# The first layer's gates by expert: built by token through DRAM before the stream, instead of by chunks between its tiles

## The chip, the core and the metric

The kernel runs on one core of a Trainium2 chip. The metric is the device time of one execution in microseconds (us), here the median of three runs. The core's engines work side by side, each through a fixed order of its own instructions: TensorE (PE; its loads of weights are PEld), VectorE (DVE), ScalarE (ACT), GpSimd (POOL) and SyncE (SP), which only starts transfers. An instruction starts when the one before it on its engine is done and when the semaphores that it waits for are set.

## The reference, cut to what matters

Two layers are computed on 256 latent tokens (LAT) and 256 context tokens (CTX) of width 1024. A layer is a mixer (a projection, a gated delta rule as a scan, pooling and Fourier groups) and then a retrieval of experts, to which the change belongs:

```python
def _peer(h, w_query, sub_keys, expert_u, expert_v):
    q = (h @ w_query).reshape(t, 8, 2, 128)
    scores = einsum('thpc,hpnc->thpn', q, sub_keys)
    s_top, i_top = top_k(scores, 16)
    cand = s_top[:, :, 0, :, None] + s_top[:, :, 1, None, :]
    cand_idx = i_top[:, :, 0, :, None] * 128 + i_top[:, :, 1, None, :]
    best, pos = top_k(cand.reshape(t, 8, 256), 16)
    idx = take_along_axis(cand_idx.reshape(t, 8, 256), pos)
    gate = softmax(best)
    act = gelu(einsum('td,thkd->thk', h, expert_u[idx]))
    return einsum('thk,thkd->td', gate * act, expert_v[idx])
```

So each token has 8 x 16 = 128 chosen experts out of 128 x 128. An expert's number is a pair of keys, the first and the second, 128 of each. In the first layer both kinds of tokens retrieve; the last layer gives only the latents.

## The kernel before

The two kinds of tokens retrieve in different ways.

**Context, by gathers.** `gather_rows` fetches, for each of the 128 choices and each block of 128 tokens, the rows of u and v of each token's expert (256 gathers of 1 MB). POOL starts an indirect DMA into a buffer `uv` (L966); VectorE multiplies the u half by h and sums it to `dots` (L975); ScalarE applies gelu and the gate; VectorE adds the v half times `dots` to `acc` (L986). Of the products with h, 19 are done by POOL instead and summed by ScalarE (`PST`, `PMOD`, L971). The buffers are UVA = 3, and UVB = 1 more for the first UVN = 100 gathers.

**Latents, densely.** `stream` goes over all 128 x 128 experts in 128 tiles, one for each first key. For each it loads the tile's u and v from DRAM (0.5 MB each, SP's queue). `first` splits the tile of u into two parts (ScalarE casts `hu`, POOL subtracts to `lu`, L231), multiplies it by the tokens on TensorE (L1111 to L1113) and applies gelu to `we` (L1115). `second` follows `LAG` tiles later (17 in the first layer, 32 in the last): it splits v (`hv`, and `lv` by VectorE, L1101), multiplies `we` by the gates of this first key (VectorE, L1131), splits the result (`wh`, `wl`) and sums its product with v in PSUM (L1142). An expert that a token hasn't chosen has gate 0.

**The gates by expert.** For that, `second` needs an array of [second key, first key, token] that holds each token's 128 gates at the places of their keys. `dense_select` gives the chosen keys and gates, a choice per partition: first keys, second keys and gates of all tokens (`chosen`). A token's gates by expert are a product on TensorE over its choices: a one-hot row of each choice's second key, times a one-hot row of its first key that is scaled by the gate. Before the change this is done in two ways.

- In the first layer, `chunk` makes it for 32 first keys at a time, in SBUF, called by `second` at tiles 0, 32, 64 and 96. For eight tokens at once VectorE makes `two` (128 keys x 8 tokens, L1037), `one` (32 keys x 8, L1041) and `og` (L1046), all bf16, where the gate is in three bf16 parts (`parts`, from `dense_select`). So there are 4 x 32 = 128 such steps, each with 24 matmuls of 32 columns.
- In the last layer, `build` makes it for all first keys before the stream. For two tokens VectorE makes the one-hot rows of both keys in one f32 instruction (`oh`, L1070); the gate is multiplied in by POOL for every other pair and by ScalarE for the others (L1078). ScalarE copies the result to `gs` (L1083), which goes to DRAM (`gd`), 16 tokens at a time. `second` reads it back for eight first keys at a time (`g`).

**What sets the order.** The program is written in this order: the context's part of the first layer up to its experts' choice; the first 100 gathers; the latents' columns (`columns`, whose last instructions on VectorE make `mix`), scan, update and `dense_select`; the stream. At tile `KV` = 114 of the stream stands `context()`: the other 156 gathers, and the context's columns and scan for the last layer. Each engine's order is fixed when the program is built, by a scheduler of the language that may put an instruction ahead of others that are written earlier when its inputs and its buffers are there: so gathers and the context's part stand in between the latents' work.

## Time and profile before

| | |
|---|---|
| median of 3 runs | 3431.07 us (3430.14 to 3433.43) |
| span of the profiled execution, first to last instruction | 3421.3 us |
| mean granted clock of TensorE | 0.916 of full speed |
| TensorE busy | 2934.5 us (86%) |
| VectorE busy | 2721.9 us (80%) |
| POOL busy | 1658.3 us (48%) |
| ScalarE busy | 1407.8 us (41%) |

The profiled execution is one run under the hardware profiler. Its span leaves out what lies before the first and behind the last instruction, so it is 9.8 us under the median of the runs. The trace gives the stages: the first gather starts at 336 us; the latents' columns are done at 517; their experts' selection starts at 762, and the first chunk at 943; the first layer's stream runs to 2112, with the last gathers at 1990 and the residual at 2117; the last layer's columns for the latents run to 2292, beside the context's scan (2106 to 2297); the scan, the update and the choice of experts to 2600; `build` from 2601 to 2732; and the last layer's stream from 2750 to 3404.

A busy share is an average over these stages. An engine that is busy is not always working: an instruction's time in the records runs from its start to its end, also if it is held up in between.

### The profile page before, as it was taken

The page shows a single profiled execution, that of the slowest core. Times are in us where ns is not written, and L with a number is a line of the kernel's source. Part 1 is how long each engine was busy: PE and PEld are TensorE (multiplying, and loading weights), DVE is VectorE, ACT ScalarE, POOL GpSimd, SP SyncE. Part 2 cuts the span into 40 slices and gives each one's busy share as a digit, 9 for nine tenths or more (in the row PEclk, how much of TensorE's full clock was granted, in tenths as well). Part 3 has the DMA queues.
Part 4 walks back from the last instruction along what each step waited for, and adds up shares of the span by engine and source line. Part 5 has one row for each costly group of instructions (what it writes and reads, how often), then busy time and mean ns, then how long its engine had stood idle before and what let it go on. Part 6 is the DMA issues. An engine that isn't in the chain of part 4 may idle for free. (4 is left out here: it accounts for less than half of the span.)

```text
span 3421.3 us, 51677 instructions
## 1 busy us (share of the span) xinstructions
PE 2934.5 (86%) x19512; PEld 2488.9 (73%) x19512; DVE 2721.9 (80%) x4617; ACT 1407.8 (41%) x2648; POOL 1658.3 (48%) x976
## 2 busy tenths in 40 slices
PE   7999946768497898898899799999776899999998
PEld 4687725636386787787788677878576788899997
DVE  4535999879999999999999976643399967777777
ACT  4533334222233443344344354643235834444443
POOL 0241237732555775777677542334256732344442
PEclk9999967879687997999899899999889999999999
DMA  6603875688666876877677653252243576666664
GB/s 249 221 26 133 334 287 211 225 345 297 233 222 240 288 252 216 283 258 268 235 275 267 227 185 114 70 174 87 65 127 111 185 245 204 198 211 212 211 209 136
DMA packets 192106, 712.74 MB, mean 208 GB/s; under 512 B 18544, under 2 KB 58864, under 8 KB 157040
## 3 DMA queue, kind: packets, MB, share of 16 engines
q1 hardware_dynamic: 154992, 440.98, 38.9%
q0 software_dynamic: 36864, 268.45, 21.7%
q8 instruction: 153, 2.51, 0.3%
q14 instruction: 97, 0.79, 0.1%
HBM read 690.49 MB, written 18.87 MB: 207 GB/s over the span
## 5 line engine op out<-in xcount | busy, mean ns | idle before, releaser
L231 POOL TENSOR_TENSOR lu<-w,hu 128x1024 fp32r<-128x1024 f32 x256 | 670.5, 2619 | 512.0 <-ACT hu L1100 498.1
L1111 PE MATMUL s<-Hh,hu 128*128 128x256 f32 x2048 | 607.9, 297 | 75.4 <-ACT we L1115 63.0
L1113 PE MATMUL s<-Hh,lu 128*128 128x256 f32 x2048 | 604.2, 295 | 21.3 <-POOL lu L231 20.7
L966 POOL DMA_INDIRECT uv<-in_uv,idx x256 | 378.1, 1477 | 483.1 <-DVE acc L986 265.7
L1112 PE MATMUL s<-Hl,hu 128*128 128x256 f32 x2048 | 596.7, 291 | 0.0
L1111 PEld LDWEIGHTS s<-Hh,hu 128*128 128x128 f32 x2048 | 411.6, 201 | 93.0 <-ACT we L1115 72.2
L1113 PEld LDWEIGHTS s<-Hh,lu 128*128 128x128 f32 x2048 | 410.4, 200 | 28.3 <-POOL lu L231 26.9
L986 DVE SCALAR_TENSOR_TENSOR acc<-uv,dots,acc 128x1024 f32<-128x1024 f32 x254 | 409.9, 1619 | 14.7 <-ACT dots L980 14.5
L1112 PEld LDWEIGHTS s<-Hl,hu 128*128 128x128 f32 x2048 | 409.9, 200 | 6.9 <-issue 0.4
L1101 DVE TENSOR_TENSOR lv<-w,hv 128x1024 fp32r<-128x1024 f32 x256 | 356.3, 1392 | 59.6 <-ACT hv L1100 58.4
L1100 ACT CAST hu<-w 128x1024 fp32r<-128x1024 f32 x256 | 268.0, 1047 | 277.0 <-PE s L1112 206.6
L1131 DVE TENSOR_TENSOR we<-we,g 128x256 f32<-128x256 f32 x128 | 258.4, 2034 | 145.0 <-ACT we L1115 126.0
L975 DVE SCALAR_TENSOR_TENSOR uv<-uv,h 128x1024 f32<-128x1024 f32 x237 | 349.6, 1477 | 14.7 <-DMA uv<-in_uv,idx 14.5
L1100 ACT CAST hv<-w 128x1024 fp32r<-128x1024 f32 x256 | 267.9, 1046 | 213.8 <-PE pj L1142 169.3
L1052 PE MATMUL c<-og,two 128*128 128x32 bf16 x3072 | 234.5, 243 | 59.2 <-DVE og L1046 56.6
L1052 PEld LDWEIGHTS <-two 128*128 128x128 bf16 x3072 | 209.1, 160 | 95.0 <-issue 47.4
L979 ACT ACTIVATE dots<-dots 128x1 f32<-128x1 f32 x256 | 51.8, 203 | 519.1 <-DVE uv L975 518.5
L231 POOL TENSOR_TENSOR wl<-we,wh 128x256 fp32r<-128x256 f32 x128 | 146.5, 1146 | 122.9 <-ACT wh L1133 73.2
L1142 PE MATMUL po<-lv,wh 128*128 128x512 f32 x512 | 172.2, 418 | 29.5 <-DVE lv L1101 28.8
L1142 PE MATMUL po<-hv,wh 128*128 128x512 f32 x512 | 167.1, 407 | 15.7 <-ACT hv L1100 8.8
L231 POOL TENSOR_TENSOR C<-L,levels 128x512 f32<-128x512 f32 x96 | 135.2, 1424 | 86.9 <-PE c L665 38.1
L1142 PE MATMUL po<-hv,wl 128*128 128x512 f32 x512 | 164.3, 402 | 3.3 <-POOL wl L231 3.3
(427 smaller groups left out, 6433.3 us busy)
## 6 DMA issues: line engine op xcount, KB each, us to landing
w<-in_tab SPq DMA_DIRECT2D x512, 512.0 KB, 4.5
w<-in_wmod SPq DMA_DIRECT2D x96, 512.0 KB, 5.1
w<-in_wq SPq DMA_DIRECT2D x48, 512.0 KB, 4.6
w<-in_win SPq DMA_DIRECT2D x44, 512.0 KB, 4.7
gd<-gs SPq DMA_DIRECT2D x16, 1024.0 KB, 4.3
g<-gd SPq DMA_DIRECT2D x16, 1024.0 KB, 5.8
w<-in_wrest SPq DMA_DIRECT2D x24, 512.0 KB, 3.8
w<-in_wout SPq DMA_DIRECT2D x24, 512.0 KB, 4.9
```

The lines of the kernel that those rows point to most:

```text
L231: pool.tensor_tensor(out, x, y, op=op)
L966: pool.indirect_dma_start(out=uv, out_offset=None, in_=a[f"uv{l}"], in_offset=bass.IndirectOffsetOnAxis(ap=st["idx", b][:, j0 + i : j0 + i ...
L975: dve.scalar_tensor_tensor(uv[:, 0:D], uv[:, 0:D], 1.0, st["h2", b], op0=OP.mult, op1=OP.mult, accum_out=dots[:, i : i + 1],)
L986: dve.scalar_tensor_tensor(acc, v, dots[:, i : i + 1], acc, op0=OP.mult, op1=OP.add)
L1052: pe.matmul(p[:, t1 - t0 + t], two[:, :, t], og[:, i, :, t], start=(i == 0), stop=(i == 2))
L1100: act.copy(hi, raw)
L1101: eng(lo, raw, hi.bitcast(F32), op=OP.subtract)
L1111: pe.matmul(p, hi[:, ks], Hh[:, k], start=(k == 0), stop=False)
L1112: pe.matmul(p, hi[:, ks], Hl[:, k], start=False, stop=False)
L1113: pe.matmul(p, lo[:, ks], Hh[:, k], start=False, stop=(k == KT - 1))
L1131: dve.tensor_tensor(wt, wt, g, OP.mult)
L1142: pe.matmul(acc[b][n], x[:, ts], y[:, n * 512 : n * 512 + 512], start=(i == 0 and j == 0), stop=(i == NKEYS - 1 and j == 2),)
```

## The change

The function `chunk` is gone, with its bf16 `parts`. Both layers use a new `build`, ahead of their stream: for four tokens VectorE makes one `two` (one-hot rows of the second key, 128 x 512 f32), and for each token one `one`, an instruction that compares with the first key and multiplies by the gate, both read as a scalar per partition. The products are f32 matmuls as in the last layer before, ScalarE copies them to `gs`, and `gs` goes to DRAM. In both layers `second` reads `g` back for eight first keys at a time. In the first layer `build` is written between `dense_select` and the stream. Besides this, all 256 products with h are VectorE's, and UVA is 4 instead of 3. Comments are taken out of the whole file, which moves the line numbers.

```diff
-                    if j0 >= PST and (j0 * NB + b) % PMOD == 0:
-                        pool_tt(uv[:, 0:D], uv[:, 0:D], st["h2", b], op=OP.mult)
-                        act.activation(uv[:, 0:D], uv[:, 0:D], AF.Copy, accum_out=dots[:, i : i + 1])
-                    else:
-                        dve.scalar_tensor_tensor(
-                            uv[:, 0:D], uv[:, 0:D], 1.0, st["h2", b], op0=OP.mult, op1=OP.mult,
-                            accum_out=dots[:, i : i + 1],
-                        )
+                    dve.scalar_tensor_tensor(
+                        uv[:, 0:D], uv[:, 0:D], 1.0, st["h2", b], op0=OP.mult, op1=OP.mult, accum_out=dots[:, i : i + 1]
+                    )
...
-    UVA, UVB, UVN = 3, 1, 100  # buffers of rows fetched, and more of them for the first ones
-    PST, PMOD = 60, 7
-    OHB = (4, 10)
+    UVA, UVB, UVN = 4, 1, 100
...
-        chosen = dp("chosen", [128, 3, T]) if l else sp("chosen", [128, 3, T])
+        chosen = dp("chosen", [128, 3, T])
...
-    def chunk(parts, c, make):
...
-    def build(l, chosen, gdram, side):
+    def build(chosen, gdram, side, banks):
...
         for tg in range(T // TG):
             gs = bp("gs", [128, NKEYS, TG], 2)
...
+                t0 = tg * TG + t4
+                p = bank([128, 4, 128], banks[t0 // 4 % len(banks)])
+                two = bp("two", [128, 4, 128], 3)
+                dve.tensor_tensor(
+                    two, chosen[:, 1, t0 : t0 + 4, None].to_broadcast([128, 4, 128]),
+                    iota[:, None, :].to_broadcast([128, 4, 128]), OP.is_equal,
+                )
+                one = bp("one", [128, 4, 128], 3)
+                for t in range(4):
+                    key, gate = (chosen[:, i, t0 + t : t0 + t + 1] for i in (0, 2))
+                    dve.tensor_scalar(one[:, t], iota, key, gate, op0=OP.is_equal, op1=OP.mult)
+                    pe.matmul(p[:, t], two[:, t], one[:, t], start=True, stop=True)
                 act.copy(gs[:, :, t4 : t4 + 4].rearrange("p i t -> p t i"), p)
             nc.sync.dma_start(gdram[:, tg], gs)
         bp.close()
...
-            if l == 0:
-                if i % KC == 0:
-                    acts["g"] = chunk(gdram, i // KC, make_v)
-                g = acts["g"][:, i % KC].rearrange("p (a t) -> p a t", t=TG)
-            else:
-                if i % IG == 0:
-                    acts["g"] = make_v("g", [128, T // TG, IG, TG], 2)
-                    nc.sync.dma_start(acts["g"], gdram[:, :, i : i + IG, :])
-                g = acts["g"][:, :, i % IG]
+            if i % IG == 0:
+                acts["g"] = make_v("g", [128, T // TG, IG, TG], 2)
+                nc.sync.dma_start(acts["g"], gdram[:, :, i : i + IG, :])
+            g = acts["g"][:, :, i % IG]
...
     Hh, Hl, keys = dense_select(0, LAT, m, dp, "right")
+    gd = gdram()
+    build(keys, gd, "right", ("c0", "c1"))
...
-    sums = stream(0, keys, Hh, Hl, su, sv, LAG[0], {KV: context})
+    sums = stream(0, gd, Hh, Hl, su, sv, LAG[0], {KV: context})
...
-    build(1, keys, gd, "right")
+    build(keys, gd, "right", ("c0", "c1", "c2"))
```

How the order of VectorE moves is shown at three places. A row is line, operation, output, inputs and shape; L975 and L986 of before are L968 and L978 of the changed kernel, L1101 and L1131 are L1047 and L1072.

The first place is VectorE at the end of the latents' columns, where `mix` is made for the last time. The buffers of the gathers are numbered two apart, from uv_739 for the first one, so uv_809 is the 36th gather and uv_897 the 80th. Before:

```order
L986 SCALAR_TENSOR_TENSOR acc1_514_2412<-uv_805_3538,dots_804_3537,acc1_514_2412 128x1024
L975 SCALAR_TENSOR_TENSOR uv_807_3545,dots_806_3544<-uv_807_3545,h20_516_2415 128x1024
L986 SCALAR_TENSOR_TENSOR acc0_513_2411<-uv_807_3545,dots_806_3544,acc0_513_2411 128x1024
L975 SCALAR_TENSOR_TENSOR uv_809_3552,dots_808_3551<-uv_809_3552,h21_520_2433 128x1024
L580 TENSOR_SCALAR mix_1039_4537<-c1_1051_4567,psc_209 128x256
L975 SCALAR_TENSOR_TENSOR uv_811_3559,dots_810_3558<-uv_811_3559,h20_516_2415 128x1024
L986 SCALAR_TENSOR_TENSOR acc1_514_2412<-uv_809_3552,dots_808_3551,acc1_514_2412 128x1024
```

After:

```order
L978 SCALAR_TENSOR_TENSOR acc1_514_2410<-uv_893_3844,dots_892_3843,acc1_514_2410 128x1024
L968 SCALAR_TENSOR_TENSOR uv_895_3851,dots_894_3850<-uv_895_3851,h20_516_2413 128x1024
L978 SCALAR_TENSOR_TENSOR acc0_513_2409<-uv_895_3851,dots_894_3850,acc0_513_2409 128x1024
L968 SCALAR_TENSOR_TENSOR uv_897_3858,dots_896_3857<-uv_897_3858,h21_520_2431 128x1024
L293 TENSOR_REDUCE mod0_80<-s_1282_5464 128x8
L978 SCALAR_TENSOR_TENSOR acc1_514_2410<-uv_897_3858,dots_896_3857,acc1_514_2410 128x1024
L577 TENSOR_SCALAR mix_1039_4535<-c1_1051_4565,psc_209 128x256
```

The last column of `mix` stood behind the product of the 36th gather, and stands behind that of the 80th now.

The second place is VectorE where the first layer's gates are made: `two`, `one` and `og` of `chunk` before, `two` and `one` of `build` after. Before, from the first chunk:

```order
L975 SCALAR_TENSOR_TENSOR uv_16581,dots_16580<-uv_16581,h_516_2415 128x1024
L1037 TENSOR_TENSOR two_7195<-parts_6497,spots 128x1024
L1041 TENSOR_TENSOR one_7197<-parts_6497,spots 128x256
L1037 TENSOR_TENSOR two_7225<-parts_6497,spots 128x1024
L1041 TENSOR_TENSOR one_7227<-parts_6497,spots 128x256
L1101 TENSOR_TENSOR lv_8189<-w_8186,hv_8188 128x1024
L1101 TENSOR_TENSOR lv_8244<-w_8241,hv_8243 128x1024
L986 SCALAR_TENSOR_TENSOR acc_513_2411<-uv_16581,dots_16580,acc_513_2411 128x1024
L1046 TENSOR_TENSOR og_7199<-one_7197,parts_6497 128x768
L1046 TENSOR_TENSOR og_7229<-one_7227,parts_6497 128x768
```

After, from the start of `build`:

```order
L1020 TENSOR_TENSOR two_6502<-chosen_5647,iota 128x512
L1027 TENSOR_SCALAR one_6504<-iota,chosen_5647 128x128 x4
L1020 TENSOR_TENSOR two_6515<-chosen_5647,iota 128x512
L1027 TENSOR_SCALAR one_6517<-iota,chosen_5647 128x128 x4
L1020 TENSOR_TENSOR two_6528<-chosen_5647,iota 128x512
L1027 TENSOR_SCALAR one_6530<-iota,chosen_5647 128x128 x4
L968 SCALAR_TENSOR_TENSOR uv_13825,dots_13824<-uv_13825,h_520_2431 128x1024
L1020 TENSOR_TENSOR two_6541<-chosen_5647,iota 128x512
L1027 TENSOR_SCALAR one_6543<-iota,chosen_5647 128x128 x4
L968 SCALAR_TENSOR_TENSOR uv_13832,dots_13831<-uv_13832,h_516_2413 128x1024
```

Before, the steps of the first chunk stand between tiles of v (`lv`) and gathers. Now the steps of `build` stand together, with a gather's product at times in between, and 34 gathers and all of `build` are ahead of the first `lv`.

The third place is VectorE in the stream, while gathers are left (`lv` and `we` are a tile of v, `uv` and `acc` a gather). Before:

```order
L1101 TENSOR_TENSOR lv_8849<-w_8846,hv_8848 128x1024
L986 SCALAR_TENSOR_TENSOR acc_513_2411<-uv_16794,dots_16793,acc_513_2411 128x1024
L1131 TENSOR_TENSOR we_8789<-we_8789,gs_7193 128x256
L1101 TENSOR_TENSOR lv_8904<-w_8901,hv_8903 128x1024
L1131 TENSOR_TENSOR we_8844<-we_8844,gs_7193 128x256
L975 SCALAR_TENSOR_TENSOR uv_16809,dots_16808<-uv_16809,h_516_2415 128x1024
L1101 TENSOR_TENSOR lv_8959<-w_8956,hv_8958 128x1024
L1131 TENSOR_TENSOR we_8899<-we_8899,gs_7193 128x256
L986 SCALAR_TENSOR_TENSOR acc_514_2412<-uv_16801,dots_16800,acc_514_2412 128x1024
L986 SCALAR_TENSOR_TENSOR acc_513_2411<-uv_16809,dots_16808,acc_513_2411 128x1024
L1101 TENSOR_TENSOR lv_9014<-w_9011,hv_9013 128x1024
```

After:

```order
L1072 TENSOR_TENSOR we_9490<-we_9490,g_10264 128x256
L978 SCALAR_TENSOR_TENSOR acc_514_2410<-uv_14357,dots_14356,acc_514_2410 128x1024
L1047 TENSOR_TENSOR lv_9495<-w_9492,hv_9494 128x1024
L968 SCALAR_TENSOR_TENSOR uv_14364,dots_14363<-uv_14364,h_516_2413 128x1024
L1047 TENSOR_TENSOR lv_9550<-w_9547,hv_9549 128x1024
L978 SCALAR_TENSOR_TENSOR acc_513_2409<-uv_14364,dots_14363,acc_513_2409 128x1024
L1072 TENSOR_TENSOR we_9545<-we_9545,g_10264 128x256
L968 SCALAR_TENSOR_TENSOR uv_14371,dots_14370<-uv_14371,h_520_2431 128x1024
L978 SCALAR_TENSOR_TENSOR acc_514_2410<-uv_14371,dots_14370,acc_514_2410 128x1024
L968 SCALAR_TENSOR_TENSOR uv_14378,dots_14377<-uv_14378,h_516_2413 128x1024
L1072 TENSOR_TENSOR we_9600<-we_9600,g_10264 128x256
```

Eight tiles of v had 8 or 9 gathers among them before and have 13 now, until all 256 are through, which is at tile 36 of v.

## Rows read from the trace of the kernel before

**Rows 1.** windows by stage: us; busy PE, PEld, DVE, ACT, POOL; clock; DMA share; GB/s.

```profile
336.00:517.00 181.00, 131.31 (x543) 92.01 (x543) 179.05 (x598) 65.13 (x162) 61.57 (x43) 0.82 0.84 316
517.00:762.00 245.00, 170.08 (x905) 127.56 (x904) 209.70 (x275) 79.30 (x229) 147.41 (x101) 0.79 0.70 257
762.00:943.00 181.00, 118.42 (x575) 92.38 (x576) 176.09 (x595) 44.82 (x105) 73.11 (x42) 0.80 0.74 267
943.00:1990.00 1047.00, 913.10 (x7157) 804.96 (x7156) 987.47 (x1001) 430.62 (x835) 716.68 (x382) 0.90 0.73 251
1990.00:2117.00 127.00, 119.82 (x628) 98.75 (x626) 76.69 (x139) 63.24 (x114) 32.44 (x31) 1.00 0.50 160
2117.00:2292.00 175.00, 167.45 (x1218) 142.09 (x1222) 106.54 (x213) 87.62 (x168) 63.08 (x50) 1.00 0.33 100
2600.00:2750.00 150.00, 121.69 (x942) 113.18 (x942) 131.40 (x132) 119.55 (x229) 106.64 (x80) 0.99 0.50 176
2750.00:3404.00 654.00, 650.28 (x3980) 581.38 (x3981) 490.86 (x510) 268.24 (x331) 246.88 (x102) 1.00 0.65 205
```

**Rows 2.** timeline of POOL and VectorE: start us, us.

```profile
1483.84 2.85 POOL L231 TENSOR_TENSOR lu<-w,hu 128x1024 fp32r<-128x1024 f32 x1 [0.77 <-ACT hu L1100]
1484.34 2.76 DVE L1046 TENSOR_TENSOR og<-one,parts 128x768 bf16<-128x768 bf16 x1
3005.36 2.40 POOL L231 TENSOR_TENSOR lu<-w,hu 128x1024 fp32r<-128x1024 f32 x1 [3.84 <-ACT hu L1100]
3005.59 2.45 DVE L1131 TENSOR_TENSOR we<-we,g 128x256 f32<-128x256 f32 x1 [1.80 <-ACT we L1115]
```

**Rows 3.** lines in 943 to 1990 us: count, ns min/median/max.

```profile
L986 DVE SCALAR_TENSOR_TENSOR acc<-uv,dots,acc x141: 1267/1282/4175, 943.6 to 1988.0; 128x1024 f32<-128x1024 f32 x141
L975 DVE SCALAR_TENSOR_TENSOR uv<-uv,h x121: 1207/1217/4117, 945.1 to 1984.5; 128x1024 f32<-128x1024 f32 x121
L1101 DVE TENSOR_TENSOR lv<-w,hv x107: 1209/1222/6993, 950.1 to 1986.9; 128x1024 fp32r<-128x1024 f32 x107
L1131 DVE TENSOR_TENSOR we<-we,gs x123: 408/415/2637, 1066.5 to 1989.2; 128x256 f32<-128x256 f32 x123
L1046 DVE TENSOR_TENSOR og<-one,parts x128: 541/548/6210, 955.8 to 1915.6; 128x768 bf16<-128x768 bf16 x128
L1037 DVE TENSOR_TENSOR two<-parts,spots x128: 673/682/3410, 946.5 to 1915.0; 128x1024 bf16<-128x1024 bf16 x128
L1041 DVE TENSOR_TENSOR one<-parts,spots x128: 275/283/3590, 949.1 to 1912.2; 128x256 bf16<-128x256 bf16 x128
L966 POOL DMA_INDIRECT uv<-in_uv,idx x139: 936/1691/4374, 941.6 to 1969.0; - x139
L231 POOL TENSOR_TENSOR lu<-w,hu x116: 2346/2696/3502, 946.2 to 1988.1; 128x1024 fp32r<-128x1024 f32 x116
L231 POOL TENSOR_TENSOR wl<-we,wh x108: 720/926/6229, 1067.4 to 1983.1; 128x256 fp32r<-128x256 f32 x108
```

**Rows 4.** small VectorE instructions with a scalar by partition, whole trace.

```profile
L496 DVE TENSOR_SCALAR y<-xpad,convw x44: 340/349/1374, 61.0 to 2222.2; 128x256 f32<-128x256 f32 x44
L846 DVE TENSOR_SCALAR start<-row x24: 114/171/2348, 317.8 to 2587.4; 128x32 f32<-128x32 f32 x24
```

**Rows 5.** timeline, VectorE, last layer's first weighting: start, us, [idle before, releaser].

```profile
2749.61 2.78 DVE L1131 TENSOR_TENSOR we<-we,g 128x256 f32<-128x256 f32 x8 [17.35 <-DMA g<-gd]
```

**Rows 6.** windows of line 986 alone, one instruction for each gather.

```profile
336.00:517.00 181.00, 44.46 (x33) 0.82 0.84 316
517.00:762.00 245.00, 84.91 (x55) 0.79 0.70 257
762.00:943.00 181.00, 37.35 (x26) 0.80 0.74 267
```

**Rows 7.** the page: mean GB/s moved in 40 equal slices.

```profile
GB/s 249 221 26 133 334 287 211 225 345 297 233 222 240 288 252 216 283 258 268 235 275 267 227 185 114 70 174 87 65 127 111 185 245 204 198 211 212 211 209 136
```

**Rows 8.** windows, the context's columns of the first layer.

```profile
43.00:140.00 97.00, 95.61 (x633) 74.75 (x634) 53.46 (x141) 51.48 (x103) 7.35 (x5) 1.00 0.56 184
```

55 lines of the change are left out of this document (removed).

## The prediction

> **What bounds the kernel now.** I read the windows by stage first [rows 1]. From 2750 us TensorE is busy for 650 of 654 us at granted clock 1.00: the last layer's stream is TensorE's. The first layer's stream, 943 to 1990 us, is not: TensorE 913 of 1047 us at clock 0.90, VectorE 987, POOL 717. VectorE looks like the bound, but its busy time is not its own. In the timeline [rows 2] an `og` of VectorE starts 0.50 us after a `lu` of POOL, takes 2.76 us where its median is 0.55 [rows 3], and ends 0.41 us after that `lu`; in the last layer a `we` starts 0.23 us into a `lu` of 2.40 us and ends 0.28 us after it. The two engines take turns in such instructions. So I treat VectorE and POOL as one resource ("the pair") and price its work by the undisturbed durations, minimum or median, of [rows 3]: a gather is POOL's issue 0.94, the product with h 1.22, the sum into `acc` 1.28, together 3.44 us; a step of a chunk (eight tokens) is `two` 0.68, `one` 0.28, `og` 0.55, together 1.51; a pair of tiles is `lu` 2.35, `wl` 0.72, `lv` 1.22, `we` 0.41, together 4.70.
>
> Check on the stream: 141 gathers 485, 128 steps 193, 116 `lu` 273, 107 `lv` 131, 123 `we` 50, 108 `wl` 78, and 19 products on POOL, in place of VectorE, some 21 more: 1231 us of work in 1047 us. A factor of 0.85, the same work, fills the stage. The pair is the limit there, TensorE second.
>
> **The change, part by part.**
>
> *Removed:* the chunks' steps, 193 us of pair work or 164 us of time by the factor, and 3072 small matmuls that TensorE had room for. The 19 products on POOL go back to VectorE: -21, or -18.
>
> *Added, first layer:* per four tokens one `two` (128x512; the old `oh` of that shape has 0.68 as its minimum in the last layer, the same as `two` now) and four `one` of 128x128. No row has that shape; the nearest are 128x32 at 0.17 and 128x256 at 0.35 [rows 4]. Between these ends I take 0.25, a little above the size's share, since two scalars by partition are read. 64 x 0.68 + 256 x 0.25 = 108 us of pair work (ends 87 and 133). ScalarE's 64 copies replace 64 others of 512 columns and are hidden: it is busy 431 of 1047 us. Each `we` now reads `g` from DRAM: 16 + 16 transfers of 1 MB on SP's queue, ahead of which and behind which the tiles' loads stand; the first `we` waits for the last write and a read. In the last layer VectorE waits 17.35 us for that read after its build [rows 5]; here the gathers between hide it.
>
> A rule bears on the small `one`: one 128x32 tensor_scalar in [rows 4] took 2.35 us, as long as a `lu`, so this form waits for POOL too, and I count it as pair work. [...] If the form did not wait, the 64 us could lie beside POOL's work and the sum would fall by up to 54 us. [...]
>
> *Moved:* this decides it. VectorE works in the order written, and with a fourth buffer (and the chunks gone) the gathers stand earlier in it. Counted in the two orders, 80 instead of 36 stand ahead of the last `mix` column of the latents, and 163 instead of 115 ahead of the first `two`. Before, 35, 55 and 26 ran in the three stages up to 943 us ([rows 6]; the first sum of each block is another instruction, so the row has 33). In the first of these VectorE is busy 179 of 181 us [rows 1]: nothing hides 45 more. Each costs VectorE 2.5 us, and up to 0.94 for POOL's issue: 3.1 x 45 = 140 us (ends 113 and 155). DMA nearly says the same: 316 GB/s of a best slice of 345 [rows 7]; 57 MB more than 45 MB in 57 + 45 = 102 MB need 296 us against 181, +115. In the second stage two fewer, -6; in the third five more, +15. So the latents' experts are chosen 149 us later, at 1092.
>
> From there to the first `lv` the order has 34 gathers, the build and about 18 `lu`: (117 + 108 + 42) x 0.85 = 227 us, to 1319. Then 13 gathers per eight tiles instead of 8 or 9: (13 x 3.44 + 8 x 4.70) x 0.85 = 70 us per eight; 36 tiles take 315 us, to 1634. There the gathers are through, 356 us earlier than now, but only 38 tiles of v and 56 of u are done, against 107 and 125.
>
> The rest is TensorE's. In the last layer 654 us hold 128 tiles of v and 103 of u: 2.83 us a tile [rows 1]. 90 + 72 tiles cost 458. The context's part of the last layer now lies inside: TensorE is busy 120 us in 1990 to 2117, of which 24 tiles are 68, so 52 are the context's columns; and 167 in 2117 to 2292, of which the latents' columns are 96 (the same code took 97 us for the context in the first layer, TensorE 95.6 [rows 8]), so 72 are its scan. 458 + 124 = 582, at the 0.95 that TensorE reached in 1990 to 2292: 613. The stream ends at 2247 instead of 2117, and the latents' columns need 97 + 17 instead of 175, because the context's scan is no longer beside them: 2361 instead of 2292, **+69**.
>
> *Last layer:* its build loses POOL's product and ScalarE's 128 scalings; TensorE has 28 us idle in 2600 to 2750. In the new order 23 tiles of u stand up to the first v there instead of 16. TensorE then needs 70 (the build, unchanged) + 65 + 17 of waiting = 152, to 2752, and has 224 tiles behind it instead of 231: 634, to 3386 instead of 3404. **-18**, at most -28.
>
> Sum: 3421.3 + 69 - 18 = 3472 of span. The median, 3431.1, is 9.8 above the span; with that, **3482 us**.
>
> **Rivals.**
>
> *The pair stays the limit to the end (faster).* If TensorE were as well fed as now, the time would follow the pair's work alone: -193 - 21 + 108 = -106, times 0.85 = -90, and -18: about 3323; half of it, with some of the shift, 3375. For it: the pair bounds 1047 us now. Against: after 1634 the pair has only 72 x 2.35 + 90 x 2.35 = 381 us of tiles for TensorE's 582. It decides if the gathers end before 1634 - 51 = 1583: then the sum is below the present time. An undisturbed `one`, or gathers at 2.5 instead of 3.1 us in the first stage (-27), together do it.
>
> *DMA takes the pair's place (slower still).* In the 36 tiles with gathers 13 + 8 + 1 MB come per eight tiles, 23 MB in 70 us: 330 GB/s, where the best slice has 345 [rows 7]. Should transfers reach only the 267 of the third stage [rows 1], eight tiles take 86 us: +72 here and some +40 before, about 3590.
>
> *It balances (same).* The shift of 69 less what a quicker build and a better filled second stage (VectorE idle 35 us there) give back: 3431.
>
> *The chunk was never in the way (the removal does nothing by itself).* TensorE at 913 of 1047 us speaks for it, the factor against; the time would then be the shift alone, +149 less the 61 that the columns save: over 3500, within the second rival's range.
>
> **How the numbers follow.** Forecast 0.52 (3440 to 3530), DMA or a stalled tail 0.18 (3530 to 3600), faster 0.22 (3330 to 3424), same 0.08 (within 0.2%, 7 us, about what a measurement of this kernel can tell). Slower is 0.70. To leave out no more than 0.2, the range takes in half of the faster case and most of the second rival: 3385 to 3570. Its ends are the bounds as well: `one` and the early gathers at their cheap ends without waiting give 3482 - 21 x 0.85 - 27 - 46, about 3390.
>
> **What would show it.** Right: no idle on VectorE in the latents' columns and 80 gathers by their end; chosen near 1090; eight tiles in 65 to 75 us, then 45 to 50 once the gathers are through, with granted clock 1.00 and TensorE at 95%; the context's scan done before the last v; the last layer's first `we` a few us earlier at most after its selection. Wrong: experts chosen before 1050; VectorE and POOL no longer taking turns in the build; idle TensorE in the tail; DMA waits ahead of the product with h.

## The result, and the profile after

The changed kernel takes 3468.05 us (median of four runs, 3461.97 to 3473.88), the kernel before 3432.25 in the same comparison. The ratio is 1.0107, with a 95% interval of 1.0092 to 1.0122: 36 us or 1.1% slower. The forecast was 3482, which is 51 us above the 3431 of before. In the profiled executions the span grew by 46.4 us, from 3421.3 to 3467.7, where the working gave 3472. The changed kernel's profiled run took 3469.49 us, 1.8 more than its span. So most of the 9.8 us that the prediction put around the span is no time outside it: the profiled execution of before was a quick one; the quickest of the kernel's timed runs in a later comparison, 3423.2 us, fits that span.

The page of the changed kernel first: busy time and share of each engine, then PE and DVE in 40 slices, then GB/s in the slices (before: [rows 7]).

```profile
PE 2838.7 (82%) x16952; PEld 2403.4 (69%) x16952; DVE 2546.9 (73%) x4780; ACT 1392.7 (40%) x2502; POOL 1490.1 (43%) x893
PE   7997408787847647777999999899776899999998
DVE  4536998797999997788655545564479987777777
GB/s 243 216 31 161 264 338 342 296 226 307 332 276 237 275 314 318 287 302 265 216 193 183 173 156 140 105 186 140 64 95 122 182 243 201 207 204 208 212 211 136
```

VectorE now has a stretch in the middle, slices 20 to 29, at 4 to 6 tenths, where TensorE is mostly at 9; ahead of it, in slices 7 to 19, TensorE is at 4 to 8. The bandwidth has its high slices early, and falls when the gathers are through.

The stages show the same in numbers. These are windows of the changed kernel, with the columns of [rows 1]: the latents' columns with the gathers; scan and update; selection; the build up to the first `lv`; the stream with gathers; the stream without; the last layer's columns; its build; its stream.

```profile
332.00:650.00 318.00, 158.32 (x600) 110.67 (x599) 287.90 (x774) 107.38 (x283) 133.14 (x91) 0.73 0.87 327
650.00:880.00 230.00, 170.77 (x916) 124.06 (x916) 199.16 (x272) 76.45 (x224) 146.89 (x97) 0.82 0.71 265
880.00:1068.00 188.00, 120.63 (x566) 93.62 (x566) 182.22 (x608) 44.68 (x113) 78.38 (x47) 0.79 0.77 287
1068.00:1287.00 219.00, 142.37 (x824) 131.12 (x824) 215.86 (x426) 93.76 (x160) 87.97 (x49) 0.73 0.75 273
1287.00:1640.00 353.00, 251.04 (x1283) 215.04 (x1284) 288.66 (x269) 119.94 (x263) 223.48 (x128) 0.85 0.85 298
1640.00:2228.00 588.00, 583.99 (x3706) 520.83 (x3706) 324.68 (x316) 304.09 (x465) 305.76 (x209) 1.00 0.51 171
2228.00:2332.00 104.00, 93.53 (x605) 74.52 (x605) 65.24 (x173) 53.86 (x105) 9.32 (x10) 0.95 0.45 145
2653.00:2813.00 160.00, 137.98 (x1042) 133.52 (x1041) 144.85 (x320) 88.11 (x109) 51.23 (x21) 0.92 0.50 177
2813.00:3448.00 635.00, 634.07 (x3866) 565.58 (x3865) 478.59 (x510) 260.80 (x320) 237.96 (x97) 1.00 0.62 207
```

In the latents' columns VectorE is busy for 288 of 318 us, where it was busy for 179 of 181: it is idle for 30 us, half of it in waits of `acc` for `dots` of ScalarE. From 650 to 880 and from 880 to 1068 it is about as full as before. From 1068 to 1640 TensorE is idle for 179 of 572 us, and from 1640 to 2228 it is busy for 584 of 588. The two limits stand one behind the other.

The sums of the gathers (L978, L986 before) answer to [rows 6]: 78 in the first stage instead of 33, 53 instead of 55, 31 instead of 26.

```profile
332.00:650.00 318.00, 104.00 (x78) 0.73 0.87 327
650.00:880.00 230.00, 73.97 (x53) 0.82 0.71 265
880.00:1068.00 188.00, 42.02 (x31) 0.79 0.77 287
```

The small `one` in the build answers to [rows 2]. Of the five rows of the timeline, the third is POOL's.

```profile
1111.19 1.10 DVE L1027 TENSOR_SCALAR one<-iota,chosen 128x128 f32<-128x128 f32 x4
1113.36 0.08 DVE L968 DVE_READ_ACCUMULATOR uv<-uv,h 128x1 f32 x1
1113.85 2.41 POOL L230 TENSOR_TENSOR lu<-w,hu 128x1024 fp32r<-128x1024 f32 x1 [2.37 <-ACT hu L1046]
1113.97 3.14 DVE L1027 TENSOR_SCALAR one<-iota,chosen 128x128 f32<-128x128 f32 x4
1117.03 0.68 DVE L1020 TENSOR_TENSOR two<-chosen,iota 128x512 f32<-128x512 f32 x1
```

Four `one` take 1.10 us when nothing is in the way, and 3.14 when a `lu` of POOL starts 0.12 us ahead of them. Of the 512 `one` of the trace's two builds 30 last over 0.5 us, and each of these overlaps a `lu` of POOL; of the other 482, 12 overlap arithmetic of POOL.

The first weighting in the last layer waits 12.23 us for `g`, instead of 17.35 [rows 5]:

```profile
2813.29 2.95 DVE L1072 TENSOR_TENSOR we<-we,g 128x256 f32<-128x256 f32 x7 [12.23 <-DMA g<-gd]
```

The moments below are from the traces, in us from the start of each; "experts chosen" is the start of ScalarE's first copy into `chosen`, "columns" is the end of the last pooled column of the latents in the last layer (L580, L577 of the changed kernel; the stage that the prediction ends at 2292 runs on to the start of the scan, 21 us later), and a weighting is L1131, or L1072 of the changed kernel. The moments of `lv` and of the weightings are starts. The rows of the experiments are explained in the next section.

| kernel | last `mix` | experts chosen | first `lv` | last gather | last `lv`, first layer | columns | first weighting, last layer | last weighting | median of runs |
|---|---|---|---|---|---|---|---|---|---|
| before | 518 | 941 | 950 | 1989 | 2112 | 2271 | 2750 | 3400 | 3432 |
| changed | 650 | 1068 | 1287 | 1640 | 2222 | 2332 | 2813 | 3447 | 3468 |
| e1 three buffers | 519 | 940 | 1141 | 1965 | 2114 | 2270 | 2761 | 3395 | 3417 |
| e2 five early, three late | 657 | 1070 | 1266 | 1835 | 2199 | 2328 | 2810 | 3443 | 3465 |
| e3 fourth buffer late only | 520 | 941 | 1155 | 1764 | 2177 | 2299 | 2780 | 3413 | 3445 |
| e4 before, five early | 655 | 1069 | 1087 | 1854 | 2234 | 2381 | 2849 | 3499 | 3521 |
| e5 e1, old build last | 521 | 941 | 1140 | 1964 | 2112 | 2268 | 2747 | 3398 | 3424 |
| e6 e1, half the gates by ScalarE | 521 | 944 | 1133 | 1966 | 2105 | 2268 | 2753 | 3380 | 3403 |
| e7 e1, `lu` on VectorE | 522 | 944 | 1138 | 1792 | 1999 | 2147 | 2631 | 3265 | 3287 |
| e8 e1, `wl` on VectorE | 522 | 943 | 1142 | 1933 | 2090 | 2253 | 2741 | 3375 | 3398 |
| e9 changed, `lu` on VectorE | 652 | 1084 | 1285 | 1556 | 2158 | 2266 | 2747 | 3381 | 3406 |
| e10 before, `lu` on VectorE | 524 | 949 | 959 | 1846 | 2028 | 2181 | 2652 | 3302 | 3322 |
| e11 e6, e7 and e8 together | 521 | 945 | 1126 | 1760 | 1957 | 2106 | 2581 | 3209 | 3232 |
| e12 e11, `lu` on VectorE twice | 522 | 950 | 1131 | 1768 | 1965 | 2112 | 2576 | 3203 | 3214 |

### The profile page after: what moved, and what is told of

Same layout as the page of the kernel before. It is cut to its first block, busy times and chain, and to the rows that moved or that the text cites. A ratio compares the mean times of both kernels' runs of the same rounds, so it can differ in the third digit from the quotient of the medians.

```text
span 3467.7 us, 46531 instructions
## 1 busy us (share of the span) xinstructions
PE 2838.7 (82%) x16952; PEld 2403.4 (69%) x16952; DVE 2546.9 (73%) x4780; ACT 1392.7 (40%) x2502; POOL 1490.1 (43%) x893
## 5 line engine op out<-in xcount | busy, mean ns | idle before, releaser
L230 POOL TENSOR_TENSOR lu<-w,hu 128x1024 fp32r<-128x1024 f32 x256 | 640.9, 2505 | 731.6 <-ACT hu L1046 705.0
L1057 PE MATMUL s<-Hh,hu 128*128 128x256 f32 x2048 | 620.5, 303 | 84.5 <-ACT we L1061 59.3
L1072 DVE TENSOR_TENSOR we<-we,g 128x256 f32<-128x256 f32 x256 | 413.4, 1628 | 280.4 <-ACT we L1061 259.2
L1047 DVE TENSOR_TENSOR lv<-w,hv 128x1024 fp32r<-128x1024 f32 x256 | 338.8, 1324 | 149.2 <-ACT hv L1046 149.0
L978 DVE SCALAR_TENSOR_TENSOR acc<-uv,dots,acc 128x1024 f32<-128x1024 f32 x254 | 374.0, 1477 | 41.3 <-ACT dots L972 41.2
L968 DVE SCALAR_TENSOR_TENSOR uv<-uv,h 128x1024 f32<-128x1024 f32 x256 | 358.5, 1403 | 19.1 <-DMA uv<-in_uv,idx 19.1
L1028 PE MATMUL c<-one,two 128*128 128x128 f32 x1024 | 178.6, 327 | 83.0 <-DVE one L1027 82.5
L1028 PEld LDWEIGHTS c<-one,two 128*128 128x128 f32 x1024 | 159.9, 234 | 95.8 <-ACT dots L972 30.9
L1027 DVE TENSOR_SCALAR one<-iota,chosen 128x128 f32<-128x128 f32 x512 | 205.7, 464 | 0.0
L1029 ACT COPY gs<-c 128x512 f32<-128x512 f32 x128 | 131.0, 1053 | 139.1 <-PE c L1028 135.7
L230 POOL TENSOR_TENSOR wl<-we,wh 128x256 fp32r<-128x256 f32 x128 | 125.9, 984 | 106.0 <-ACT wh L1074 77.4
```

Source lines behind the costliest of these rows:

```text
L230: pool.tensor_tensor(out, x, y, op=op)
L968: dve.scalar_tensor_tensor(uv[:, 0:D], uv[:, 0:D], 1.0, st["h2", b], op0=OP.mult, op1=OP.mult, accum_out=dots[:, i : i + 1])
L978: dve.scalar_tensor_tensor(acc, v, dots[:, i : i + 1], acc, op0=OP.mult, op1=OP.add)
L1028: pe.matmul(p[:, t], two[:, t], one[:, t], start=True, stop=True)
L1047: eng(lo, raw, hi.bitcast(F32), op=OP.subtract)
L1057: pe.matmul(p, hi[:, ks], Hh[:, k], start=(k == 0), stop=False)
```

## The experiments

Theory A is the prediction's: the gathers that moved ahead are the loss, because VectorE and POOL, which take turns, limit the first part, and TensorE alone the rest. The rivals put the loss on the build itself (B), on the density of gathers in the stream alone (C), or on the later choice of experts alone (D).

### Gathers and gates taken apart (e1 to e4)

**e1: the changed kernel with three buffers.**

```diff
-    UVA, UVB, UVN = 4, 1, 100
+    UVA, UVB, UVN = 3, 1, 100
```

> The changed kernel with UVA = 3 instead of 4, as before; all else as changed. In its order 35 gathers stand ahead of the last mix column (80 with four buffers), 115 ahead of the first two (163), 141 ahead of the first lv (197), and 8 to 10 among eight tiles instead of 13, so that the last gather stands at tile 104 of v instead of 36. Theory A (the gathers moved forward are the loss; they leave TensorE idle early and alone late): experts chosen at 943, first lv at about 1141, gathers through near 1975, stream's end near 2190, latents' columns of the last layer done at 2299, the end 7 us later than before there and 14 us given back in the last layer: 3425 us (3405 to 3440). Theory B (the build ahead of the stream is the loss, since no tile of v runs during it; the buffers do little): 3468, within 10 us.

Measured: 3417.48 us (3413.69 to 3424.14), ratio to before 0.9962 (0.9947 to 0.9977). The first `lv` came at 1141, as worked out. The build does not lose time: with the gathers where they were, the changed kernel is 0.4% faster than before, and 51 us faster than with four buffers. B falls.

**e2: five buffers for the first 100 gathers, three afterwards.**

```diff
-    UVA, UVB, UVN = 4, 1, 100
+    UVA, UVB, UVN = 3, 2, 100
```

> The changed kernel with UVA = 3, UVB = 2: five buffers for the first 100 gathers as in the changed kernel, three afterwards as before. Its order has 80 gathers ahead of the last mix column, but 8 or 9 among eight tiles of the stream, the last at tile 69 of v. Theory A: chosen at 1068 as in the changed kernel, first lv at 1266, the gathers through at 1821 with 69 tiles of v and 86 of u done; 101 tiles at 2.83 and the context's 124 us are left for TensorE: stream's end 2231 and the whole 3468 (3455 to 3480). Theory C (the 13 gathers among eight tiles are the loss, not the shift of the choice): near the kernel with three buffers, under 3440. Theory B: 3468.

Measured: 3465.48 us (3456.12 to 3465.84), ratio 1.0092 (1.0073 to 1.0111), the gathers through at 1835. It is as slow as the changed kernel, though the gathers are no denser in the stream than with three buffers. C falls as the only cause. Against e1 the early gathers cost 48 us.

**e3: the fourth buffer from the 101st gather on.** Its early gathers are those of before.

```diff
-    UVA, UVB, UVN = 4, 1, 100
+    UVA, UVB, UVN = 3, 1, 100
...
             return extra("uv", [128, 2 * D], UVB)
+        if n >= UVN and n % (UVA + UVB) >= UVA:
+            return late[0]("uv", [128, 2 * D], UVB)
...
     extra.close()
+    late = [Stage("uv")]
...
+        late[0].close()
         steady.close()
```

> The changed kernel with three buffers and the extra one for the first 100 gathers, as before, and a fourth one only from gather 101 on. Its order has 35 gathers ahead of the last mix column and 120 ahead of the first two, but 13 among eight tiles, the last at tile 64. Theory A: chosen at 943, first lv at 1162, 78 us for eight tiles as measured in the changed kernel, the gathers through at 1780 with 64 tiles of v and 81 of u done; then 111 tiles at 2.83 and 124 us of the context: stream's end 2218, the whole about 3455 (3440 to 3470), since gathers that crowd the stream's first half cost what they cost ahead of it. Theory D (only the later choice of experts is the loss): as with three buffers, 3425. Theory B: 3468.

Measured: 3445.17 us (3436.25 to 3447.11), ratio 1.0043 (1.0027 to 1.0059). Experts are chosen as early as before, and yet 28 of the 51 us are lost. Gathers that crowd the stream's first half cost, too. D falls as the only cause; the size was overrated by 10 us.

**e4: the kernel before, with five buffers for the first 100 gathers.**

```diff
-    UVA, UVB, UVN = 3, 1, 100
+    UVA, UVB, UVN = 3, 2, 100
```

> The kernel before, chunks and all, with UVB = 2 instead of 1, that is five buffers for the first 100 gathers and three afterwards. Its order has 80 gathers ahead of the last mix column (35 before) and 154 ahead of the first chunk (116), with 8 among eight tiles as before. Theory A: chosen at 1070, gathers through near 1870 at tile 78 of v, stream's end near 2249, latents' columns done near 2353 instead of 2292: 3493 us (3470 to 3510) without any change to the gates. Theory B (the build, not the gathers): 3432, within 10 us.

Measured: 3520.7 us (3518.95 to 3527.97), ratio 1.0266 (1.0247 to 1.0284). Without any change to the gates the early gathers alone cost 88 us. That is 28 us more than expected, and outside the range. The choice came at 1069 as worked out, the last gather at 1854 for 1870, the last `lv` at 2234 with the stream's end expected at 2249; the miss lies in the columns, from 2239 to 2381 us, 142 instead of the 104 that were taken over from the changed kernel: 160 products of the context's scan (L665, L668) still lie among them.

So the change has two parts: the swap of chunks for the build at equal buffers (15 us faster at three buffers, e1; 55 faster at five early ones, e2 against e4), and the fourth buffer (51 slower). The swap as measured here holds the last layer's new build and the 19 products that went back to VectorE as well; no run tests the products by themselves. The costs of the fourth buffer don't add up either: early gathers alone cost 48 us (e2), a denser stream alone 28 (e3), both together 51.

Why is the swap worth only 15? The prediction counted 193 us of chunk steps and 21 of products less, and 108 of the build more, which by its factor are 90 us of time; e1's gathers are through only 24 us earlier. These are e1's windows: its build, the stream with gathers, and then without.

```profile
941.00:1141.00 200.00, 137.91 (x821) 129.26 (x820) 193.97 (x399) 89.61 (x142) 71.18 (x40) 0.74 0.71 254
1141.00:1965.00 824.00, 662.12 (x3640) 557.74 (x3641) 677.95 (x569) 308.30 (x638) 537.43 (x317) 0.93 0.84 294
1965.00:2117.00 152.00, 148.99 (x822) 126.77 (x821) 89.95 (x151) 84.41 (x140) 52.06 (x43) 0.98 0.47 150
```

VectorE is busy 678 of 824 us instead of 793 of 849; it waits now. Its chain of waits in e1, from 1141 to 1965 us (us in total, times, longest):

```profile
DVE lv L1047 <- ACT hv L1046: 65.3, 49, 2.9
DVE acc L978 <- ACT dots L972: 61.3, 55, 2.1
```

and that of the kernel before, 1141 to 1990:

```profile
DVE lv L1101 <- ACT hv L1100: 27.6, 24, 2.5
DVE two L1037 <- PE c L1052: 11.2, 9, 4.7
DVE acc L986 <- ACT dots L980: 8.6, 11, 4.0
```

`lv` and `acc` wait 127 us for ScalarE in e1's 824 us, and 36 in 849 before. So the chunks' steps seem to have filled gaps in VectorE's order, in which a `hv` or a `dots` was on its way; this is read from the waits, and no run takes these waits away alone. And POOL holds VectorE up. In this timeline of e1 one `lv` takes 5.71 us where its median is 1.22 [rows 3], because POOL does two `lu` in 4.68 us:

```profile
1535.64 5.71 DVE L1047 TENSOR_TENSOR lv<-w,hv 128x1024 fp32r<-128x1024 f32 x1 [1.56 <-ACT hv L1046]
1535.59 4.68 POOL L230 TENSOR_TENSOR lu<-w,hu 128x1024 fp32r<-128x1024 f32 x2
```

### The last layer's build (e5)

**e5: e1 with the old build in the last layer.** `build` of before stands beside the new one, and the last layer calls it.

```diff
-    build(keys, gd, "right", ("c0", "c1", "c2"))
+    build_old(1, keys, gd, "right")
```

> The kernel with three buffers (the changed kernel with UVA = 3), and in the last layer the old build: oh for two tokens, the gate by POOL and ScalarE. The first layer keeps the new build. Theory A: the choice of the last layer at 2601 in both; the old build ends about 12 us earlier (first weighting of v at 2750 instead of 2761), but 16 instead of 23 tiles of u stand ahead of it, so 651 instead of 635 us follow: 5 us slower than with three buffers, 3422 (3414 to 3430); the last layer's new build is then worth 5, and the first layer's swap of chunks for build the other 10. Rival: the later first weighting is lost for good: 11 us faster, 3406.

Measured: 3424.31 us (3415.06 to 3432.61), ratio 0.9982 (0.9972 to 0.9992), against 0.9962 for e1. The first weighting came 14 us earlier than in e1, and the last one 2.5 us later: TensorE has done 30 tiles of u before the first weighting in e1 and 25 in e5, so more tiles of u ahead give back what the longer build takes. The rival, 3406, falls. The two intervals overlap; that the new build is worth some 5 us in the last layer is likely, not shown.

### Less work on VectorE, and POOL out of its way (e6 to e8)

**e6: e1, half of the gates multiplied in by ScalarE.**

```diff
+                split = t0 // 4 % 2
+                if split:
+                    dve.tensor_tensor(
+                        one, chosen[:, 0, t0 : t0 + 4, None].to_broadcast([128, 4, 128]),
+                        iota[:, None, :].to_broadcast([128, 4, 128]), OP.is_equal,
+                    )
                 for t in range(4):
                     key, gate = (chosen[:, i, t0 + t : t0 + t + 1] for i in (0, 2))
-                    dve.tensor_scalar(one[:, t], iota, key, gate, op0=OP.is_equal, op1=OP.mult)
+                    if split:
+                        act.activation(one[:, t], one[:, t], AF.Copy, scale=gate)
+                    else:
+                        dve.tensor_scalar(one[:, t], iota, key, gate, op0=OP.is_equal, op1=OP.mult)
```

> The kernel with three buffers; in build, every other group of four tokens makes one by a single 128x512 is_equal on VectorE and ScalarE multiplies the gate in, 0.39 for each token. On VectorE such a group costs 2 x 0.60 instead of 0.60 + 4 x 0.257 from start to start: 14 us less in each build. Theory A: 13 less in the first layer, where VectorE and POOL are the limit during the build, and 5 in the last layer, where TensorE has 22 us idle during it: 3400 (3392 to 3412). Rival: during the builds ScalarE or TensorE limits as well: 3417 within 6, or slower where ScalarE (88 busy of 160 us there, and 50 more) holds up the casts of u.

Measured: 3402.74 us (3400.84 to 3405.4), ratio 0.9918 (0.9906 to 0.9931), 15 us under e1. The size is right, its place is not: the columns are done 2 us earlier than in e1, and the other 13 came in the last layer, where 5 were expected. The last layer's build in e6, and the same window of e1:

```profile
2601.00:2755.00 154.00, 143.36 (x1114) 135.44 (x1113) 134.60 (x224) 125.31 (x242) 62.48 (x24) 0.99 0.59 198
```

```profile
2601.00:2755.00 154.00, 132.47 (x997) 128.30 (x995) 144.47 (x320) 85.37 (x104) 47.24 (x19) 0.91 0.49 174
```

TensorE is busy for 143 instead of 132 us there, at granted clock 0.99 instead of 0.91. In the first layer the build did become shorter, as expected: from the choice to the first `lv` it is 188 us instead of 200. But the gathers were through no earlier than in e1 (1966 for 1965), so little of it was left at the end of the stream.

**e7: e1, `lu` of the first layer subtracted by VectorE.**

```diff
-            hi, lo = table(i, 0, "u", pool_tt, make_u)
+            hi, lo = table(i, 0, "u", pool_tt if l else dve.tensor_tensor, make_u)
```

> The kernel with three buffers; in the first layer lu is subtracted by VectorE (as lv is, 1.22 us) and no longer by POOL (2.35). Theory A (VectorE and POOL take turns in these instructions, so only the sum of both counts): 1.13 less for each of 128 tiles, 145 us of the pair's work; the gathers through earlier by 50 to 100 us, of which the waits on ScalarE and TensorE's own work leave some 50: 3367 (3320 to 3400). Rival (the two engines work beside each other and VectorE is the limit): VectorE gets 99 x 1.22 = 121 us more in the 824 us from the first lv to the last gather, where it is busy 678 and waits 146: 50 to 120 us slower, 3470 to 3540.

Measured: 3287.18 us (3285.93 to 3295.11), ratio 0.9588 (0.9572 to 0.9603). VectorE got 128 instructions more, and the kernel became 130 us faster; the rival had it 50 to 120 slower. So the two engines do not just work beside each other. The gain was underrated by 80 us, and lies outside the expected range. What shows the turns themselves is how long VectorE's instructions last in the stretch from the first `lv` to the last gather (count | busy us, mean ns | idle before), in e1:

```profile
L978 DVE SCALAR_TENSOR_TENSOR acc<-uv,dots,acc 128x1024 f32<-128x1024 f32 x115 | 238.5, 2074 | 61.3 <-ACT dots L972 61.3
L1072 DVE TENSOR_TENSOR we<-we,g 128x256 f32<-128x256 f32 x119 | 106.3, 905 | 19.4 <-ACT we L1061 13.8 <-ACT dots L971 5.3
```

and in e7:

```profile
L978 DVE SCALAR_TENSOR_TENSOR acc<-uv,dots,acc 128x1024 f32<-128x1024 f32 x110 | 148.3, 1349 | 5.2 <-ACT dots L972 5.2
L1072 DVE TENSOR_TENSOR we<-we,g 128x256 f32<-128x256 f32 x111 | 48.3, 447 | 20.5 <-ACT we L1061 18.3 <-POOL wl L230 1.8
```

The medians of [rows 3] are 1.28 and 0.42 us. What lies above them, for these two, the product with h and `lv` together, is some 240 us in e1 and some 25 in e7. But e7 does more than shorten the turns: TensorE gets a `lu` after 1.22 us (the median) instead of at least 2.35 [rows 3], and POOL no longer has `lu` between the gathers that it starts. How the 130 us divide among these three, no run shows. The windows of e7's build, stream with gathers, and stream without:

```profile
944.00:1138.00 194.00, 126.05 (x731) 116.99 (x729) 182.00 (x415) 87.46 (x139) 40.87 (x28) 0.73 0.75 270
1138.00:1792.00 654.00, 576.70 (x3352) 502.19 (x3353) 550.78 (x630) 294.29 (x595) 269.80 (x204) 0.95 0.95 347
1792.00:1999.00 207.00, 206.95 (x1248) 181.44 (x1248) 113.41 (x188) 121.59 (x192) 53.95 (x54) 0.99 0.49 159
```

From the first `lv` to the last gather it is 654 us for 95 tiles of v and 110 gathers, instead of 824 for 103 and 115: 55 us for eight tiles, instead of 64. Transfers reach 347 GB/s at a share of 0.95. In e1 they stood at 294.

**e8: e1, `wl` of the first layer subtracted by VectorE.**

```diff
-            (dve.tensor_tensor if l else pool_tt)(wl, w, wh.bitcast(F32), op=OP.subtract)
+            dve.tensor_tensor(wl, w, wh.bitcast(F32), op=OP.subtract)
```

> The kernel with three buffers; in the first layer wl is subtracted by VectorE (0.41 us, as we) and no longer by POOL (0.72). Theory A: 0.31 less for each of 128 tiles, 40 us of the pair's work, of which half may show: 3397 (3380 to 3415). Rival (the engines work beside each other): VectorE gets 52 us more: 3440 to 3470.

Measured: 3397.8 us (3382.96 to 3402.68), ratio 0.9894 (0.9871 to 0.9917). That is 20 us faster than e1, as worked out; the rival, 3440 to 3470, falls.

### Does the loss of the fourth buffer come from the turns? (e9, e10)

**e9: the changed kernel, four buffers, with e7's edit.**

```diff
-            hi, lo = table(i, 0, "u", pool_tt, make_u)
+            hi, lo = table(i, 0, "u", pool_tt if l else dve.tensor_tensor, make_u)
```

> The changed kernel with its four buffers, and lu of the first layer on VectorE. Theory A: the experts are chosen as late as in the changed kernel (1068), since nothing of lu lies ahead; first lv at about 1283; 50 gathers are left, 12 or 13 among eight tiles, now limited by transfers at the 343 GB/s seen with lu on VectorE: 67 us for eight tiles, through at 1551 with 32 tiles of v and 49 of u done; then 175 tiles at 2.83 and 124 us of the context for TensorE alone: stream's end 2176, the whole 3418 (3400 to 3435). So a fourth buffer costs some 130 us against three (3287), more than the 51 with lu on POOL. Rival (the fourth buffer hurt because VectorE and POOL were in each other's way): it costs 20 or less now, 3290 to 3310.

Measured: 3406.09 us (3402.72 to 3408.26), ratio 0.9929 (0.9913 to 0.9946). The fourth buffer costs 119 us against e7, more than with `lu` on POOL. Its windows, the stream with gathers and without:

```profile
1285.00:1556.00 271.00, 205.90 (x1140) 170.85 (x1141) 227.05 (x266) 102.92 (x228) 120.78 (x82) 0.92 0.95 342
1556.00:2163.00 607.00, 606.82 (x3857) 541.25 (x3856) 321.10 (x402) 315.43 (x482) 154.23 (x140) 1.00 0.53 174
```

For 607 us TensorE works without a gap, and in the 271 before it was idle for 65. So the turns are not what makes the fourth buffer cost: with `lu` off POOL it costs more, and the loss is where the gathers stand (e2, e3). One step of the expectation failed: the choice came at 1084 us, not 1068. `lu` does lie ahead of it: VectorE had made 12 `lu` and 170 gathers' sums by then, where in the changed kernel it had made 163 sums and POOL 8 `lu`.

**e10: the kernel before, with e7's edit.** The line is the same in it.

> The kernel before, with chunks and three buffers, and lu of the first layer on VectorE. Theory A: 145 us less of the pair's work there, some 100 of time by the pair's factor, and TensorE had 141 idle in 943 to 2117: 3330 (3305 to 3360); the swap of chunks for the build is then worth 20 to 50, more than the 13 with lu on POOL, since the waits that took the place of the chunks' steps are filled. Rival: VectorE, which has the chunks' 193 us as well, is the limit alone: little gained, over 3390.

Measured: 3321.7 us (3313.4 to 3325.21), ratio 0.9674 (0.9656 to 0.9693), 109 us faster than before. The swap of chunks for the build is worth 35 us here (e7), more than the 15 with `lu` on POOL, as expected.

### The version that beats both (e11, e12)

**e11: e6, e7 and e8 together.**

```diff
+                    if split:
+                        act.activation(one[:, t], one[:, t], AF.Copy, scale=gate)
...
+            hi, lo = table(i, 0, "u", pool_tt if l else dve.tensor_tensor, make_u)
...
+            dve.tensor_tensor(wl, w, wh.bitcast(F32), op=OP.subtract)
```

> Three buffers, the new build with half of the gates multiplied in by ScalarE, and both lu and wl of the first layer on VectorE. Theory A: the pair has another 40 + 28 us less, but transfers are at 343 GB/s and TensorE at 611 of 704 us between the first lv and the last gather, so a part of it: 3268 (3250 to 3285). Rival: the gains add up as measured alone, 15 and 20 under 3287: 3252.

Measured: 3232.16 us (3221.45 to 3246.21), ratio 0.9425 (0.9391 to 0.946). Both theories fail: it is 20 us faster than the sum of its parts (3252), and 36 faster than Theory A had it. The 20 us came in the first layer: the columns are done 41 us earlier than in e7, where e6 and e8 alone gave 2 and 17. Why the three help each other, no run shows.

**e12: e11, and `lu` on VectorE in the last layer too.**

```diff
-            hi, lo = table(i, 0, "u", pool_tt if l else dve.tensor_tensor, make_u)
+            hi, lo = table(i, 0, "u", dve.tensor_tensor, make_u)
```

> The kernel of e11, with lu on VectorE in the last layer too, so that POOL subtracts no tile any more. Theory A: VectorE's 477 busy of 652 us in that stream are mostly time held up by lu (a weighting of v takes 2.4 us there instead of 0.41), so there is room; but TensorE is busy 646 of the 652 and 135 of the 147 us of the build, so at most 13 to 18 us can come back: 3222 (3210 to 3235). Rival: VectorE's busy time is its own, and 103 to 128 more lu of 1.22 make it 603 to 633 of 652: waits in the stream, 5 to 40 us slower, 3237 to 3272.

Measured: 3214.3 us (3212.08 to 3226.01), ratio 0.9367 (0.935 to 0.9384), 18 us faster than e11 and inside the expected range; the rival falls. The weightings of the last layer (count, ns min/median/max) and its stream's window, e11 first:

```profile
L1081 DVE TENSOR_TENSOR we<-we,g x128: 406/2452/2621, 2581.4 to 3208.5; 128x256 f32<-128x256 f32 x128
2560.00:3212.00 652.00, 646.26 (x3926) 576.27 (x3925) 477.21 (x517) 268.76 (x337) 242.09 (x97) 0.99 0.63 206
```

and e12, with the first layer's stream ahead of the last layer's:

```profile
L1081 DVE TENSOR_TENSOR we<-we,g x128: 414/418/427, 2576.3 to 3203.0; 128x256 f32<-128x256 f32 x128
1100.00:1760.00 660.00, 572.20 (x3389) 493.01 (x3390) 565.27 (x751) 302.92 (x621) 180.86 (x113) 0.96 0.96 355
2560.00:3202.00 642.00, 627.36 (x3805) 559.24 (x3805) 397.06 (x601) 261.04 (x324) 0.00 (x0) 0.99 0.64 205
```

A weighting takes 0.42 us instead of 2.45, and VectorE, with all of `lu` in addition, is busy 397 instead of 477 us. Five sixths of a weighting's busy time was time in which it was held up.

## Why the prediction was right, step by step

The forecast came true in its direction, its size and most of its mechanism. That the span of 3472 us was met within 5 is in part luck: up to the last layer's scan the prediction's loss was some 16 us too large, and behind it its gain was 11 us too large.

**The limit of the first layer's stream: right.** VectorE and POOL take turns in these instructions: the sum into `acc` lasts 2.07 us in the mean in e1's stream, 1.35 with `lu` off POOL (e7), and the median in the kernel before is 1.28 [rows 3]; a weighting in the last layer lasts 2.45 us in the median with `lu` on POOL (e11), and at most 0.43 with `lu` off it (e12).

**The price of the build: right.** From the start of one `one` to that of the next it is 0.257 us, from a `two` to its first `one` 0.60. So a group of four tokens is 0.60 + 4 x 0.257 = 1.63 us and 64 of them 104, where the sum had 108. The duration in the records, 0.336, overlaps the next one: a `one` starts some 0.08 us before the record of the one ahead of it ends, not at that end. The 0.25 was the author's estimate between the two sizes of [rows 4], and the start-to-start time agrees with it; that reading two scalars adds to it, as the prediction has it, no run shows.

**The shift of the experts' choice: right, 22 us too large.** It is +127 us instead of +149. In the latents' columns it was 132 for 140 (45 gathers at 2.9 instead of 3.1 us), in the second stage -15 for -6, in the third +9 for +15. One sign failed: VectorE is idle for 30 of the 318 us of the columns, where the prediction wanted none.

**The factor of 0.85: held for the build, failed after it.** From the choice to the first `lv` it was 219 us for 227. But eight tiles with 13 gathers took 87, 73, 76 and 76 us instead of 70: the stretch with gathers, 353 us, is 0.94 of the pair's work as the prediction prices it, not 0.85. VectorE waits there for ScalarE (23 us before `lv`, 20 before `acc`). The prediction took a factor from a stretch in which the chunks' steps were there to fill such gaps. That the gathers were through at 1640 us for 1634 is luck: a first `lv` 32 us early met a stretch 38 us too long.

**The rest as TensorE's: right.** From 1640 to 2228 TensorE is busy for 584 us, where the prediction had 582 from there to the stream's end, and for 0.99 of the time, not 0.95. The residual behind the stream starts at 2231 us, for 2247 (2117.7 before). The stage that the prediction ends at 2292 runs to the start of the latents' scan, which in the trace of before and in that of the changed kernel is

```profile
2292.43 0.68 DVE L633 TENSOR_TENSOR L<-c,mask_l 128x512 f32<-128x512 f32 x1
```

```profile
2345.88 0.69 DVE L630 TENSOR_TENSOR L<-c,mask_l 128x512 f32<-128x512 f32 x1 [0.19 <-DVE mixl L247]
```

So from the residual to the scan it is 115 us for 114, since the context's scan was over by then (its last sum is at 2224), and the scan starts 53 us later than before, for +69.

**The last layer: -7 us for -18, a step that failed.** From the scan's start to the end of the span the changed kernel is 7 us quicker. The prediction took TensorE as the limit of the last layer's build, and so had 152 us from the choice to the first weighting, 2 more than before. It took 161, where before it was 149. VectorE sets this time: it works through its steps of the build almost without a break (145 us busy of 148), for 148 us instead of 131, and then waits 12 us for `g` instead of 17. By the prediction's own prices its work there grows too, from 128 `oh` at 0.68, 87 us, to 108; the sum for the last layer has no term for it. The largest wait of TensorE from the choice to the first weighting, before and after (us in total, times, longest):

```profile
PE c L1082 <- ACT gs L1083: 21.4, 26, 2.6
```

```profile
PE c L1028 <- DVE one L1027: 20.5, 13, 2.3
```

It is for VectorE now, and was for ScalarE's copies. The tiles of u ahead gave 17 us back, for 20: 64 us later at the first weighting, and 46 at the last one. e6 agrees with this: with less of the build on VectorE, 13 us came back in the last layer.

**The gap around the span: wrong by 8 us,** as told above; with 2 instead of 9.8 the working gives 3474 against the 3468 measured. Between the medians the change is +36 us for +51.

**The other signs.** Eight tiles without gathers took 34 to 66 us, for 45 to 50, with granted clock 1.00 as forecast. VectorE and POOL still take turns in the build (four `one` took 3.14 us instead of 1.10 beside a `lu`), and TensorE is not idle in the tail (busy for 584 of 588 us).

**The rivals.** That the pair is the limit to the end did not come about, since TensorE is busy for 584 of the last 588 us of the stream; at three buffers its sign was right (e1), its size not: 15 us of 90. DMA as a limit did not show in the changed kernel, which moved 298 GB/s in the stretch with gathers, where no product with h waits for its rows, while e7 and e12 moved 347 and 355 in theirs. "The chunk was never in the way" is half true: at three buffers the swap gives 15 us, with the pair relieved 35. For the 46 in the lower end of its range the prediction shows no sum: by the prediction's own 54 for a `one` that doesn't wait, and the 27 of the gathers, that end is 3401.

## What to carry to other kernels

A buffer more for a prefetch also moves the prefetched work ahead in the consumer's order (here the kernel with four buffers is 51 us slower than with three, e1); count what now stands ahead of the work that the next stage waits for, and ask which engine will be alone at the end (here TensorE, for 588 us). Where two engines work in the same stretch and one of them has instructions with a maximum far above the median (here `lv`, 6.99 us and 1.22 [rows 3]), price their work by the undisturbed durations and as one sum: moving an instruction to the engine with the higher busy share made the kernel 130 us faster here (e7). A factor of overlap that is taken from a stretch need not hold where that stretch's filler work is gone: it was 0.85 with the chunks' steps, and 0.94 without them.

## What the runs showed of the hardware that was not expected

- Moving 128 subtractions of 128x1024 from POOL (2.35 us) to VectorE (1.22) gave 130 us, 1.0 us for each (e1 to e7), though VectorE was the busier of the two before and after: 678 us against POOL's 537 in e1's stream with gathers, 551 against 270 in e7's.
- In the last layer's stream the weighting fell from 2.45 to 0.42 us in the median when POOL did nothing any more (e11 to e12), with no change to the instruction itself.
- With POOL relieved, gathers and tiles moved 347 GB/s (e7) and 355 (e12), at a DMA share of 0.95 to 0.96, in the mean over some 655 us; the best slice of 85 us before was 345 [rows 7].
- In the first layer's build TensorE, busy for 142 of 219 us, had a granted clock of 0.73 in the mean: 1.00 from 1080 to 1100 us, 0.50 from 1268 to 1285. In the stretch from 1640 us on, busy for 584 of 588, it had 1.00 in the mean.
